# Expert turns of a mixture of experts: seven on 64-row blocks with unsplit weights, third weights unsplit in all, a third set of weight buffers

## The chip, the cores and the metric

The kernel runs on one core of one Trainium2 chip. The metric is the device time of one execution in microseconds (us); the time given for the kernel before is the median of three runs.

## The reference

One inference step through two trunk layers for 512 prompt tokens and 64 sample tokens (8 sequences of 8), 576 tokens of 1,024 features in all. A layer is a mixer (three head groups) with a norm, and then a hierarchical mixture of experts with a second norm. The change touches the experts alone:

```python
def hier_moe(h, l, p):
    ...
    combine = jnp.sum(jax.nn.one_hot(expert_idx, MOE_EXPERTS, dtype=F32) * w_top[..., None], 1)
    hid = jax.nn.silu(jnp.einsum('nd,edf->nef', t, p['moe_w1'][l])) * \
        jnp.einsum('nd,edf->nef', t, p['moe_w3'][l])
    y = jnp.einsum('nef,efd->nd', hid * combine[..., None].astype(hid.dtype), p['moe_w2'][l])
```

There are 16 experts; every token goes to two of them. An expert's weights are w1 and w3 (1,024 x 256 each) and w2 (256 x 1,024), 1 MB apiece in float32. How many tokens an expert gets follows from the inputs, and can be counted by evaluating the reference on them: in layer 0 the experts have 41, 7, 50, 12, 11, 106, 60, 143, 99, 48, 186, 103, 75, 25, 64 and 122 tokens, in layer 1 they have 3, 4, 9, 10, 31, 64, 82, 3, 13, 70, 88, 15, 76, 215, 291 and 178.

## The kernel before, in words

**Work.** `experts` (L1660 on) runs the experts of a layer one after the other, in 16 turns b = 0 to 15. Turns 0 and 1 are experts 0 and 1; the others come by rank, in the order of `RANK`, a table that sets light experts between full ones. Turn 2 holds the fullest of the others, turns 5 and 8 the next two. A turn's `Block` takes up to 128 tokens' rows. An expert with more than 128 tokens has a second block `b2` on the same weights, one with more than 256 a third, `b3`; these stand under `tc.If`, and every engine branches round them when they aren't needed. By the counts above, second blocks run in turns 2 and 5 of layer 0 and in turns 2, 5 and 8 of layer 1, and one third block in turn 2 of layer 1: 18 blocks in layer 0 and 20 in layer 1.

**A block's steps.** `gather` (L1301, POOL's queue): an indirect DMA fetches the rows. `turn` (L1313): PE transposes them in eight pieces, ACT (L1316) and DVE (L1317) write them as a pair of float32r tiles, high and low part. `up(0)`, `up(1)` (L1324): the products with w1 and w3; each takes 24 matmuls of 256 columns, since both sides are pairs: high x high, high x low and low x high, over 8 pieces of 128 features. ACT's silu (L1326) closes `up(0)`, a DVE product (L1328) `up(1)`. `hid` (L1334): two transposes, and a pair again (L1336, L1337). `down` (L1348 to L1350): 12 matmuls of 512 columns with w2's pair, then ACT (L1354) and DVE (L1356) write the weighted rows to `ys`. `scatter` (L1360, POOL's queue): an indirect DMA adds the rows to `ybuf` in DRAM. Scatters of one expert may overlap; a scatter waits for that of the expert before, since both may add to the same row.

**Weights.** Each 1 MB piece is loaded by SP (`expert_piece`, L1270) and split into a pair by ACT (L317, high part) and DVE (L318, low part):

```python
split.hi = act.activation(hi[:, :n], raw[:, :n], AF.Copy)
dve.tensor_tensor(lo[:, :n], raw[:, :n], hi[:, :n].bitcast(F32), op=ALU.subtract)
```

There are two sets of three raw buffers, `wraw` and `slots`; turns take them alternately. Four places for pairs (pools `wsp`, `w2p`).

**Order.** The loop `for b in range(NE + 1)` in `experts` is a software pipeline: in turn b it issues `up(0)` of b, the split of w2 of b - 1, the load of w2 of b + 1, the split of w1 of b + 1, the loads of w1 and w3 of b + 2, `up(1)` of b, the conditional blocks, `turn` of b + 1, `gather` of b + 2, the split of w3 of b + 1, `down` and `scatter` of b - 1, and `hid` of b. Buffers are double: rows, `ys` and hidden tiles by b % 2. The last two turns' rows take another way to the next norm. `ahead` loads and splits the first weights of the next layer's projection.

Of the kernel before, what the change touches and what calls it, by code (L numbers as in the profile page):

```python
# [44 lines left out]
# second norm: the tiles to which the last two experts' rows come from the chip, all tiles in order  # L45
# [3 lines left out]
# when the groups of the modulation (layer, group) are worked out: beside SSD, GLA, the output projection of either layer  # L49
# [10 lines left out]
def _tables():  # L60
# [46 lines left out]
    # a token's number - 1023, in two parts  # L107
    put("tok", np.stack([np.tile(p[:, None] - 127, (1, 5)), np.tile(128 * np.arange(5) - 896, (128, 1))], 2))
    put("iota384", np.tile(np.arange(384.0), (128, 1)))
    # rows (table, expert): what tells equal counts apart, the expert's own column, ranks of the columns (table, turn), the expert  # L110
# [5 lines left out]
    put("expert", e[:, None])  # L116
    put("iota256", np.tile(np.arange(256.0), (128, 1)))
# [33 lines left out]
def _body(nc, tc, a, ctx, dbg):  # L151
# [16 lines left out]
    class Views:  # L168
        """a pool's tiles as pieces of one tile."""
# [28 lines left out]
    # the last constants are loaded where they are used  # L198
# [31 lines left out]
    # per-layer modulation held feature-major for the mixer input: [f, k, (shift, 1+scale), 9]  # L230
# [8 lines left out]
    def ada_steps(l, g):  # L239
        """one piece of a group's columns after the other."""  # L240
        # quadrants: group 0 (shift, scale) of the mixer; 1 (shift, gate); 2 (scale, gate), the gate that of the columns before
# [19 lines left out]
        if g == 2:  # L261
            # the norm's gain and bias meet the experts' scale and shift
# [11 lines left out]
            # the prompt's, feature-major  # L274
# [506 lines left out]
    def gla(l, gp, q, k, v, la, lac, gates):  # L781
# [1464 lines left out]
```

## Time and profile before

| | |
|---|---|
| median of three runs | 1490.86 us (1490.02 to 1493.58) |
| span of the profiled execution, first to last instruction | 1487.9 us |
| PE busy | 1235.3 us, 83% |
| DVE busy | 1015.5 us, 68% |
| ACT busy | 606.0 us, 41% |
| POOL busy | 499.1 us, 34% |
| DMA moved | 258.50 MB |

Busy time is summed over stages of different kinds, so its share of the whole span doesn't tell what bounds a stage. The experts are read from stretches of the trace: layer 0's lie between 478 and 711.4 us, layer 1's between 1187 and 1440 us. The start of a turn's silu (L1326 on ACT) follows its `up(0)` and serves as a mark of the turn. A group's row gives what it takes, the idle time of the engine before it and what ended that; a granted clock of 1.0 is 2.4 GHz of TensorE, 0.5 is 1.2 GHz.

### The profile page before, as it was taken

What the parts mean: (1) busy time and instruction counts of PE and PEld (TensorE: products, weight loads), DVE (VectorE), ACT (ScalarE), POOL (GpSimd) and SP (SyncE); (2) the same over time, 40 slices, a digit from 0 to 9 for tenths busy, and PEclk for the clock granted to TensorE, in tenths of its full rate; (3) what the DMA queues carried; (4) which work ended last, traced back from release to release, by engine and by line L of the source; (5) the groups of instructions that cost most, each with busy time, mean ns of one, the idle gap of its engine ahead of it and who ended that gap; (6) DMA issues with size and microseconds to landing.
All of it is one profiled execution on the core that took longest, in us unless ns stands there. A gap on an engine that the chain in (4) does not pass through costs nothing. (4 is left out here: it accounts for less than half of the span.)

```text
span 1487.9 us, 23447 instructions
## 1 busy us (share of the span) xinstructions
PE 1235.3 (83%) x8446; PEld 1028.5 (69%) x8446; DVE 1015.5 (68%) x2035; ACT 606.0 (41%) x978; POOL 499.1 (34%) x354
## 2 busy tenths in 40 slices
PE   4999999988985788898489998989998578688870
PEld 0998777775764677787289887767576466677750
DVE  0576466347889867788877647446788965575887
ACT  0552233331354454666355223333134444364742
POOL 0023122224153555342252312233314363633315
PEclk7899999999976899999799998999997698999995
DMA  9545665754231555998624310017543253685952
GB/s 311 164 149 172 239 237 201 282 203 147 95 127 47 199 208 181 310 320 287 180 82 150 116 58 32 30 45 268 167 175 106 83 216 110 211 268 179 340 155 99
DMA packets 93426, 258.50 MB, mean 174 GB/s; under 512 B 25854, under 2 KB 54432, under 8 KB 74328
## 3 DMA queue, kind: packets, MB, share of 16 engines
q1 hardware_dynamic: 82136, 237.66, 45.5%
q0 software_dynamic: 11136, 18.87, 5.5%
q8 instruction: 86, 1.41, 0.4%
q14 instruction: 68, 0.56, 0.1%
HBM read 236.26 MB, written 34.70 MB: 182 GB/s over the span
## 5 line engine op out<-in xcount | busy, mean ns | idle before, releaser
L318 DVE TENSOR_TENSOR wlo<-wraw,whi 128x2048 fp32r<-128x2048 f32 x72 | 180.3, 2509 | 38.8 <-ACT whi L317 36.1
L390 PE MATMUL ps<-whi,hT 128*128 128x256 f32 (+1 forms) x640 | 186.4, 291 | 0.8 <-DVE yi L706 0.8
L391 PE MATMUL ps<-wlo,hT 128*128 128x256 f32 (+1 forms) x640 | 181.1, 283 | 1.0 <-DVE wlo L318 1.0
L392 PE MATMUL ps<-whi,hT 128*128 128x256 f32 (+1 forms) x640 | 181.1, 283 | 0.1
L317 ACT ACTIVATE whi<-wraw 128x2048 fp32r<-128x2048 f32 x72 | 137.8, 1914 | 42.2 <-PEq L1894 9.8
L1360 POOL DMA_INDIRECT ybuf<-ys,srci x34 | 88.2, 2595 | 175.4 <-DVE hidl L1337 35.4
L318 DVE TENSOR_TENSOR wlo<-slots,whi 128x2048 fp32r<-128x2048 f32 x48 | 119.2, 2491 | 16.0 <-ACT whi L317 11.8
L390 PEld LDWEIGHTS ps<-whi,hT 128*128 128x128 f32 (+1 forms) x640 | 115.8, 181 | 13.2 <-issue 10.1
L1324 PE MATMUL ps<-whi,xh 128*128 128x256 f32 x608 | 95.1, 303 | 33.9 <-DVE xl L1317 23.6
L391 PEld LDWEIGHTS ps<-wlo,hT 128*128 128x128 f32 (+1 forms) x640 | 115.6, 181 | 3.6 <-issue 2.1
L392 PEld LDWEIGHTS ps<-whi,hT 128*128 128x128 f32 (+1 forms) x640 | 115.2, 180 | 1.3 <-issue 0.8
L1324 PEld LDWEIGHTS ps<-whi,xh 128*128 128x128 f32 x608 | 83.8, 204 | 38.7 <-DVE xl L1317 25.6
L317 ACT ACTIVATE whi<-slots 128x2048 fp32r<-128x2048 f32 x48 | 92.1, 1918 | 28.5 <-PEq L1883 10.4
L1324 PE MATMUL ps<-whi,xl 128*128 128x256 f32 x608 | 89.9, 292 | 6.2 <-DVE xl L1317 6.1
L1324 PE MATMUL ps<-wlo,xh 128*128 128x256 f32 x608 | 91.8, 297 | 1.1 <-DVE wlo L318 1.1
L380 PE MATMUL ps<-hT,whi 128*128 128x288 f32 x512 | 88.5, 294 | 0.0
L1324 PEld LDWEIGHTS ps<-whi,xl 128*128 128x128 f32 x608 | 82.7, 201 | 7.2 <-DVE xl L1317 7.0
L1324 PEld LDWEIGHTS ps<-wlo,xh 128*128 128x128 f32 x608 | 84.8, 206 | 1.3 <-DVE wlo L318 1.3
L1301 POOL DMA_INDIRECT qk<-hbuf,srci x32 | 48.0, 1499 | 81.9 <-PE ps L1313 55.2
L380 PEld LDWEIGHTS ps<-hT,whi 128*128 128x128 f32 x512 | 74.6, 188 | 0.4 <-ACT zdt L519 0.4
L1482 PE MATMUL ps<-whi,mh 128*128 128x512 f32 (+1 forms) x160 | 71.1, 444 | 3.7 <-ACT mh L1468 3.7
L254 PE MATMUL ada<-wada,scond 128*32 128x512 f32 x384 | 57.2, 670 | 18.3 <-DMA wada<-w_ada 18.3
(526 smaller groups left out, 2942.2 us busy)
## 6 DMA issues: line engine op xcount, KB each, us to landing
wada<-w_ada SPq DMA_DIRECT2D x48, 1024.0 KB
wraw<-moe_w SPq DMA_DIRECT2D x48, 1024.0 KB
slots<-moe_w SPq DMA_DIRECT2D x48, 1024.0 KB
wraw<-w_in SPq DMA_DIRECT2D x24, 1024.0 KB
wraw<-w_out SPq DMA_DIRECT2D x8, 1024.0 KB
ybuf<-bz SPq DMA_DIRECT2D x8, 512.0 KB
slots<-ybuf SPq DMA_DIRECT2D x8, 512.0 KB
slots<-ln SPq DMA_DIRECT2D x6, 512.0 KB
```

Source lines behind the costliest of these rows:

```text
L254: pe.matmul(acc[32 * q:32 * q + 32, :], sc_[:, k, :], w[:, o:o + 512], start=(k == 0), stop=(k == KD - 1))
L317: split.hi = act.activation(hi[:, :n], raw[:, :n], AF.Copy)
L318: dve.tensor_tensor(lo[:, :n], raw[:, :n], hi[:, :n].bitcast(F32), op=ALU.subtract)
L380: pe.matmul(p[:mw, :], lhs[:, k, m0:m0 + mw], rhs[:, k, 288 * h:288 * (h + 1)], start=(k == 0 and lhs is vh and rhs is hT[0]), stop=(k == ...
L390: pe.matmul(p[:n], hT[0][:, k, xs], vh[:, k, :], start=(k == 0), stop=False)
L391: pe.matmul(p[:n], hT[0][:, k, xs], vl[:, k, :], start=False, stop=False)
L392: pe.matmul(p[:n], hT[1][:, k, xs], vh[:, k, :], start=False, stop=(k == KD - 1))
L1301: self.got = pool.indirect_dma_start(out=self.X[r], out_offset=None, in_=hbuf[:, :], in_offset=bass.IndirectOffsetOnAxis(ap=self.tabs[0][r ...
L1324: pe.matmul(p, x[:, k], v[:, k], start=(x is self.xh and v is vh and k == 0), stop=(x is self.xl and k == KD - 1))
L1360: st = pool.indirect_dma_start(out=ybuf[:, :], in_=self.ys[r], in_offset=None, out_offset=bass.IndirectOffsetOnAxis(ap=self.to[r], axis=0) ...
L1482: pe.matmul(p[:n], mh[:, k, :n], vh, start=(k == 0), stop=False)
```

## The change

Turns whose rank is under 2 or over 8, but not the last two, become light: `LIGHT` = turns 0, 1, 3, 4, 6, 7 and 9. The others (2, 5, 8, 10 to 15) stay as they are but for w2.

- A light turn (`class Light`) takes a block of 64 rows. Its weights and rows are plain float32 and not split. `up` has for each of the 8 pieces one matmul with w1, whose result goes to PSUM partitions 0 to 63, and one with w3 into partitions 64 to 127. `down` puts the two halves of the 1,024 output columns side by side in the same way, and one ACT operation over 128 partitions x 512 writes `ys`; the scatter has 128 half rows of 2 KB, by a table of its own (`tabs[3]`, made in `finish` with four small matmuls, one DVE and one ACT operation).
- A light expert with more than 64 tokens has a further 64-row block `bx`, one with more than 128 also the old second and third block, under a `tc.If` in each light turn. By the counts above none of the seven has more than 64 tokens in either layer (turn 9 has exactly 64 in both).
- `down` takes w2 and the hidden rows as plain float32 in every block: 4 matmuls of 512 columns, no split of w2, no L1337.
- A third set of raw buffers, `w3rd`, takes the room of the pair pool `w2p`; turn b takes set b % 3. w1 and w3 of b + 3 are loaded once `up` of a light turn b has read them, those of b + 4 once the heavy turn b + 1 is split, and w2 of b + 2 after `down` of b - 1. Pairs are left with the two places of `wsp`.

```diff
+LIGHT = [b for b in range(NE - 2) if RANK[b] < 2 or RANK[b] > 8]
...
         def up(self, i):
-            vh, vl = [w.rearrange("p (k n) -> p k n", k=KD) for w in self.w[i]]
             p = ps(256, self.pl)
...
-            vh, vl = [w.rearrange("p (f n) -> p f n", f=2) for w in self.w[2]]
+            v = self.w[2].rearrange("p (f n) -> p f n", f=2)
             for h in range(2):
                 c = slice(512 * h, 512 * (h + 1))
                 p = ps(pl=self.pl)
                 for f in range(2):
-                    pe.matmul(p, hh[:, f], vh[:, f, c], start=(f == 0), stop=False)
-                    pe.matmul(p, hh[:, f], vl[:, f, c], start=False, stop=False)
-                    pe.matmul(p, hl[:, f], vh[:, f, c], start=False, stop=(f == 1))
+                    pe.matmul(p, self.hT[:, f], v[:, f, c], start=(f == 0), stop=(f == 1))
...
+    class Light(Block):
...
+        def gather(self, r=None):
+            if not self.part:
+                return super().gather(slice(0, 64))
...
+        def turn(self):
+            p = ps(pl=self.pl)
...
+            for k in range(KD):
+                pe.transpose(p[:, 64 * k:64 * (k + 1)], self.X[0:64, 128 * k:128 * (k + 1)], ident[0:64, 0:64])
+            act.activation(self.xT, p.rearrange("p (k n) -> p k n", k=KD), AF.Copy)
+
+        def up(self):
+            v = [w.rearrange("p (k n) -> p k n", k=KD) for w in self.w[:2]]
+            p = ps(256, self.pl)
+            for k in range(KD):
+                for i in range(2):
+                    pe.matmul(p[64 * i:64 * i + 64], self.xT[:, k], v[i][:, k], start=(k == 0), stop=(k == KD - 1))
+            sl, slp = self.sl[0:64], self.slp[0:64]
+            act.activation(sl, p[0:64], AF.Silu)
+            dve.tensor_tensor(slp.rearrange("p f a -> p a f"), sl.rearrange("p (a f) -> p a f", f=2),
+                              p[64:128].rearrange("p (a f) -> p a f", f=2), op=ALU.mult)
...
+        def down(self):
+            v = self.w[2].rearrange("p (f n) -> p f n", f=2)
+            p = ps(pl=self.pl)
+            for f in range(2):
+                for h in range(2):
+                    pe.matmul(p[64 * h:64 * h + 64], self.hT[:, f, 0:64], v[:, f, 512 * h:512 * (h + 1)], start=(f == 0), stop=(f == 1))
+            act.activation(self.ys[:, 0:512], p, AF.Copy, scale=self.tabs[4][:, self.part, self.col:self.col + 1])
+
+        def scatter(self, r=None):
+            return self.add(ybuf[:, :].rearrange("t (h c) -> (t h) c", h=2), self.ys[:, 0:512],
+                            self.tabs[3][:, self.part, self.col:self.col + 1], 2 * T)
...
+            def room(b):
+                return [wraw.tile([128, 2048], F32, name="wraw", tag="raw") for _ in range(3)] if b % 3 == 0 else (slots[:3], w3rd)[b % 3 - 1][:]
...
             for b in range(NE + 1):
-                if b < NE:
-                    bl[b].up(0)
-                if b > 0:
-                    if b == NE:
-                        bl[b - 1].hi = lambda: pair(w2p)
-                    bl[b - 1].split(2)
-                    if 1 < b + 1 < NE:
-                        load(b + 1, 2)
-                if b + 1 < NE:
+
+                if 0 < b < NE:
+                    if b in LIGHT:
+                        bl[b].up()
+                    else:
+                        bl[b].up(0)
+                if b + 1 < NE and b + 1 not in LIGHT:
+                    raw = bl[b + 1].w
+                    bl[b + 1].w = list(raw)
                     bl[b + 1].split(0)
-                if b + 2 < NE:
-                    bl[b + 2].w = rot()
-                    for i in range(2):
-                        load(b + 2, i)
-                if b < NE:
+                if b < NE and b not in LIGHT:
                     bl[b].up(1)
...
+                if b < NE and b in LIGHT and b + 3 < NE:
+                    for i in range(2):
+                        load(b + 3, i)
                 if b + 1 < NE:
                     bl[b + 1].turn()
                     if b + 2 < NE and b + 2 not in GSPLIT:
                         bl[b + 2].gather()
-                    bl[b + 1].split(1)
+                    if b + 1 not in LIGHT:
+                        bl[b + 1].split(1)
+                        if b + 4 < NE:
+                            for i in range(2):
+                                load(b + 4, i)
...
+                if b == 0:
+                    load(2, 2)
+                elif b + 2 < NE:
+                    load(b + 2, 2)
```

**PE in layer 0, from `hid` of turn 3 to `turn` of block 5, before.** `xh`, `xl` are a block's rows, `whi`, `wlo` a weight's pair, `ps` PSUM, `cst` the identity for a transpose; `qk` holds gathered rows and the product of `up`.

```order
L1334 MATMUL ps<-cst,qk 128x128 x2
L1324 MATMUL ps<-whi,xh_4630 128x256 x8
L1324 MATMUL ps<-wlo,xh_4630 128x256 x8
L1324 MATMUL ps<-whi,xl_4631 128x256 x8
L1324 MATMUL ps<-whi,xh_4630 128x256 x7
L1837 UNCONDITIONAL_BRANCH
L1324 MATMUL ps<-whi,xh_4630 128x256
L1324 MATMUL ps<-wlo,xh_4630 128x256 x8
L1324 MATMUL ps<-whi,xl_4631 128x256 x8
L1313 MATMUL ps<-cst,qk 128x128 x8
```

The 48 matmuls are both `up` products of turn 4.

**The same engine after the change, from `up` of turn 3 to `up` of turn 4.** `xf` are a light block's rows, `wraw`, `slots` and `w3rd` raw weights, `hid` the hidden rows.

```order
L1421 MATMUL ps<-wraw,xf_4637 64x256 x16
L1413 MATMUL ps<-cst,qk 128x64 x8
L1366 MATMUL ps<-w3rd,hid_4638 128x512 x4
L1430 MATMUL ps<-cst,qk 128x64 x2
L1421 MATMUL ps<-slots,xf_4636 64x256 x15
```

Sixteen matmuls on 64 partitions stand in the place of 48, four for the `down` of the heavy turn 2 in the place of twelve. Between `up` of turn 3 and its `hid` stand the transposes of block 4 and the `down` of block 2.

**SP's queue in layer 0, the loads of one turn, before:**

```order
L1270 DMA wraw_5475<-moe_w1 128x2048
L1270 ISA
L1270 DMA wraw_5476<-moe_w3 128x2048
L1837 UNCONDITIONAL_BRANCH
L1270 ISA
L1270 DMA wraw_5477<-moe_w2 128x2048
```

These are the weights of turn 4, w1 and w3 issued in turn 2 and w2 in turn 3. **After the change, those that stand in turn 4:**

```order
L1278 DMA slots_3266<-moe_w1 128x2048
L1278 ISA
L1278 DMA slots_3266<-moe_w3 128x2048
L1903 TENSOR_LOAD ebi_3262
L1903 ISA x2
L1278 ISA
L1278 DMA w3rd_4645<-moe_w1 128x2048
L1278 ISA
L1278 DMA w3rd_4645<-moe_w3 128x2048
L1278 ISA
L1278 DMA wraw_5690<-moe_w2 128x2048
```

Five pieces stand together, for turns 7 (`slots`), 8 (`w3rd`) and 6 (`wraw`), so loads are issued two to four turns ahead of their use; before, it was one to two.

## Rows read from the trace of the kernel before

**Rows 1.** The page's head and part 1: span, busy time and share.
```profile
span 1487.9 us, 23447 instructions
PE 1235.3 (83%) x8446; PEld 1028.5 (69%) x8446; DVE 1015.5 (68%) x2035; ACT 606.0 (41%) x978; POOL 499.1 (34%) x354
```

**Rows 2.** Busy time by stretch: engines' us (instructions), granted clock, DMA share, GB/s.
```profile
478.00:711.40 233.40, 196.45 (x1268) 177.75 (x1266) 178.80 (x148) 129.94 (x139) 100.06 (x44) 0.92 0.72 244
1187.00:1440.00 253.00, 210.00 (x1376) 186.47 (x1375) 172.07 (x152) 128.28 (x144) 105.30 (x45) 0.95 0.65 222
609.80:620.70 10.90, 9.86 (x72) 9.03 (x71) 7.97 (x7) 7.72 (x8) 3.76 (x2) 1.00 1.02 325
640.60:655.10 14.50, 12.20 (x78) 11.20 (x77) 11.24 (x9) 9.61 (x9) 5.79 (x2) 0.88 1.00 354
674.30:691.10 16.80, 12.64 (x72) 11.16 (x72) 12.25 (x12) 9.75 (x9) 1.58 (x1) 0.80 1.01 339
1404.70:1418.70 14.00, 11.07 (x81) 10.07 (x80) 12.20 (x12) 9.63 (x9) 3.38 (x1) 1.00 0.97 341
609.30:702.90 93.60, 85.36 (x582) 77.93 (x581) 77.36 (x67) 63.92 (x66) 31.11 (x15) 0.95 0.92 316
```

**Rows 3.** PE's timeline, one turn of layer 0: start, us, instructions in order.
```profile
609.59 1.11 PE L1324 MATMUL ps<-whi,xh 128*128 128x256 f32 x8
610.54 1.12 PE L1324 MATMUL ps<-wlo,xh 128*128 128x256 f32 x8
611.50 1.12 PE L1324 MATMUL ps<-whi,xl 128*128 128x256 f32 x8
612.46 1.04 PE L1313 MATMUL ps<-cst,qk 128*128 128x128 f32 x8
613.25 0.48 PE L1348 MATMUL ps<-whi,hidh 128*128 128x512 f32 x1
...
616.14 0.38 PE L1334 MATMUL ps<-cst,qk 128*128 128x128 f32 x2
```

**Rows 4.** PE's timeline: plain float32 products in other stages, and their neighbours.
```profile
135.23 1.92 PE L254 MATMUL ada<-wada,scond 128*32 128x512 f32 x16
137.08 1.08 PE L669 MATMUL ps<-cst,ll 64*64 64x64 f32 x15
712.11 5.42 PE L2000 MATMUL ps<-qk,v 128*128 128x512 f32 x12 [0.75 <-DVE qk L1352]
```

**Rows 5.** Groups of layer 0's experts: busy us, mean ns, idle before and releasers.
```profile
L318 DVE TENSOR_TENSOR wlo<-wraw,whi 128x2048 fp32r<-128x2048 f32 x25 | 67.5, 2705 | 5.9 <-ACT whi L317 5.1 <-ACTq L1883 0.9
L318 DVE TENSOR_TENSOR wlo<-slots,whi 128x2048 fp32r<-128x2048 f32 x24 | 58.4, 2445 | 8.7 <-ACT whi L317 7.0 <-ACTq L1883 1.4 <-DVEq L1883 0.2
L317 ACT ACTIVATE whi<-wraw 128x2048 fp32r<-128x2048 f32 x25 | 47.9, 1917 | 15.1 <-PEq L1883 5.1 <-PEq L1894 4.3 <-DMA wraw<-moe_w 4.3
L1317 DVE TENSOR_TENSOR xl<-ps,xh 128x512 fp32r<-128x512 f32 x36 | 23.2, 681 | 5.8 <-ACT xh L1316 5.5 <-DVEq L1883 0.2
```

**Rows 6.** Who PE and ACT waited for, layer 0, then layer 1: us, times, longest.
```profile
PE ps L1324 <- DVE xl L1317: 18.7, 8, 4.7
PE ps L1324 <- DVE xl L1317: 11.0, 10, 2.9
ACT whi L317 <- DMA slots<-moe_w: 7.0, 4, 2.4
```

**Rows 7.** DMA of layer 0's experts, from 478 to 711.4 us.
```profile
DMA packets 13728, 56.90 MB, mean 244 GB/s; under 512 B 3415, under 2 KB 5591, under 8 KB 8317
```

**Rows 8.** POOL's timeline, scatters of layer 0; last, all scatters' time to landing.
```profile
621.90 2.92 POOL L1360 DMA_INDIRECT ybuf<-ys,srci  x1 [7.06 <-DVE hidl L1337]
...
667.40 2.72 POOL L1360 DMA_INDIRECT ybuf<-ys,srci  x1 [6.54 <-DMA ybuf<-ys,srci]
...
702.86 2.79 POOL L1360 DMA_INDIRECT ybuf<-ys,srci  x1 [7.66 <-DMA wraw<-w_in]
DMA to landing us min/median/max: 2.7/8.5/13.3
```

More of the change, by code (lines that the diff above doesn't have):

```diff
@@ L116, in _tables @@
     put("expert", e[:, None])
+    put("beyond", np.tile(np.array([64.0 if b in LIGHT else 128.0 for b in range(NE)]), (128, 1)))
     put("iota256", np.tile(np.arange(256.0), (128, 1)))
@@ L1305, in split @@
         def split(self, i):
[L1306 removed]
+            self.w[i] = split(self.w[i])
         def turn(self):
@@ L1652, in finish @@
             act.activation(wslot, pv[:, :, 1], AF.Copy)
+            p = ps(256)
+            for e in range(2):
+                for h in range(2):
+                    pe.matmul(p[64 * h:64 * h + 64, 32 * e:32 * e + 32], tq[:, 64 * e:64 * e + 64], perm, start=True, stop=True)
+            pv = p[:, 0:64].rearrange("p (j a e) -> p j a e", j=2, a=2)
+            dve.tensor_scalar(tabs[3], pv[:, :, 0], 2.0, C("off"), op0=ALU.mult, op1=ALU.add)
+            act.activation(tabs[4], pv[:, :, 1], AF.Copy)
             held.clear()
@@ L1770, in aside @@
                     for i in range(2):
-                        ahead.load(i)
+                        ahead.load(i, w3rd[i])
                 if b == NE - 2:
@@ L1835, in parts @@
                 h, r = HALF[b], ROWS[b]
-                if h < r and both:
+                if b not in LIGHT and h < r and both:
                     with tc.If((half & (1 << b)) > 0) as big:
@@ L1842, in parts, with whole @@
                 return [f(slice(0, r))]
+            def whole(q, w):
+                q.w = w
+                q.gather()
+                q.turn()
+                for i in range(2):
+                    q.up(i)
+                q.hid()
+                q.down()
+                q.scatter()
             steps = finish(Xs[3])
@@ L1847, in experts @@
             pool.memset(Xs[3], 0.0)
-            with two(0):
-                b2[0].gather()
-                if 0 in SOON:
-                    three(0, b3[0].gather)
             with tc.issue_after(last[0].ins), tc.issue_after(last[1].ins):
-                bl[0].split(0)
-                bl[0].split(1)
+                bl[0].up()
+            for i in range(2):
+                load(2, i)
             for i in range(2):
@@ L1892, in experts @@
                             three(b - 1, more)
-                    if b in at_hand:
+                    if b in at_hand and b in LIGHT:
+                        with two(b):
+                            q = bx[b]
+                            q.w = bl[b].w
+                            q.gather()
+                            q.turn()
+                            q.up()
+                            q.hid()
+                            q.down()
+                            q.scatter()
+                            if b in SECOND:
+                                with tc.If((second & (1 << b)) > 0):
+                                    whole(b2[b], bl[b].w)
+                                    three(b, lambda: whole(b3[b], bl[b].w))
+                    elif b in at_hand:
                         with two(b):
@@ L1939, in experts @@
             wr = slots[1]
-            his = [pair(w2p) for _ in range(2)]
             with tc.If(nx > 0), ExitStack() as sI:
```

137 lines of the change are left out of this document (85 added, 52 removed).

## The prediction

> **What bounds the kernel now.** The page's head [rows 1] says PE 83% busy over the span, but the change touches the two expert stages alone, so I went to busy time by stretch [rows 2]. Layer 0's experts take 233.4 us, layer 1's 253.0 us, a third of the span together. In both PE is the busiest engine (196.45 and 210.00 us), DVE second (178.80 and 172.07 us), and DMA stands at 0.72 and 0.65. The timeline of one turn [rows 3] gives PE's work for a block at full clock: 24 products of a piece start at 609.59 and the transposes follow at 612.46, so 2.87 us a piece and 5.74 us for two; transposes 0.8 us; twelve products of `down` from 613.25 to 616.14, 2.9 us; two transposes of `hid`, 0.25 us. That is 9.7 us. 18 blocks make 175 us in layer 0, 20 make 194 us in layer 1. Some 59 us of either stage are therefore not PE work at full speed, but waits and stretches at half clock.
>
> The plain turn 609.8 to 620.7 [rows 2] shows why a turn isn't shorter: PE 9.86 of 10.90 us, and DMA at a share of 1.02 with 325 GB/s. DVE has three splits of about 2.5 us [rows 5] and some 3 us more in a turn. So PE, DVE and DMA all need about 10 us per turn. Where a turn is longer, it is the weights that are late: 640.6 to 655.1 and 674.3 to 691.1 [rows 2] have DMA at 1.00 and 1.01 with 354 and 339 GB/s, and the granted clock falls to 0.88 and 0.80 (partly at 1.2 GHz) while PE has gaps. Layer 1 has the like at 1404.7 [rows 2]; ACT's splits there waited up to 2.4 us a time for a load [rows 6]. Other gaps of PE are the DVE's: the rows' low part stands behind splits in its queue, 18.7 us in layer 0 and 11.0 us in layer 1 [rows 6]. Last, POOL: a scatter waits for the landing of the one before. The eight from 621.90 to 702.86 [rows 8] stand 11.6 us apart (81 us over seven steps), of which landing takes 8.5 us in the median and up to 13.3.
>
> **What the change takes and adds.**
>
> *PE, light turn.* Plain float32 products cost more than float32r. The 12 matmuls that begin at 712.11 [rows 4] take 5.42 us, 0.44 us apart, and each is one of the two passes that a product of 512 columns takes: 0.87 us a product, and half of that, 0.43 us, for 256 columns. But four 32-column products on parts of the array run side by side: 16 matmuls of 512 columns in 1.92 us at 135.23 [rows 4], where one after the other they would take 7. So I take a pair of 64 columns as one: eight pairs of `up` at 0.43 us are 3.45 us, two pairs of `down` at 0.87 us are 1.73 us, transposes and `hid` 1.0 us; 6.2 us against 9.7, that is 3.5 us less in each of 7 turns, 24.5 us per layer.
> *PE, heavy block.* `down` becomes four products at 0.87 us, 3.5 us against 2.9: 0.6 us more in 11 blocks of layer 0 (nine turns, two second blocks) and 13 of layer 1, 6.6 and 7.8 us. PE's sum: 18 us less in layer 0, 17 in layer 1, 35 together.
> *Mode of the array.* A light turn goes between parts and the whole array about five times, 70 times in all. After the parts' products the next matmul starts at 137.08 [rows 4], 0.09 us after the last pass would have made room (the fourth of four steps of 0.43 us ends at 136.99). I take 0.09 us, 6 us in all; bounds 0 and 0.2 us (the 0.19 us by which the last of the 16 outlasts its step: 1.92 less four steps), so 0 to 14 us. The Trainium skill's page on TensorEngine Tiling (Array Packing), under Key Properties, says that a change of tiling mode drains the engine; this speaks against the change. [...]
> *DVE and ACT.* Of the splits [rows 5], 21 of a layer go with the light turns and 9 with the heavy ones' w2: 30 of 48, at 2.5 us on DVE 75 us and at 1.92 us on ACT 58 us; the light rows' low parts (2 x 0.68 us a block) are 9.5 us more. DVE falls from 179 to about 95 us and ACT from 130 to about 70, both well under PE. A light turn keeps one silu, one product, three copies. What DVE's queue made PE wait can mostly go; I take two thirds of 18.7 and 11.0 us [rows 6], 12 and 7 us, bounds none and all.
> *Loads.* SP's queue has the same 48 pieces, but two to four turns ahead of their use. The late turns named above exceed 9.7 us by 4.8, 7.1 and 4.3 us, and layer 0's start runs at low DMA shares while turns wait. I take 12 us in layer 0 and 10 in layer 1, bounds 0 and 25 each. The cap is DMA itself: 56.9 MB in layer 0 [rows 7] at the 316 GB/s that 93.6 us sustained [rows 2] is 180 us; with some 10 us for the last block behind its weights, layer 0 can't fall under 190 us, 43 us less than now, or at 354 GB/s 171 us, 62 less.
> *POOL.* A light turn's gather has 64 rows; its scatter 128 half rows with the same bytes. Its price isn't in the trace. From below it is 0, since the bytes are the same and no gain follows; from above, 4.8 us more (the 13.3 us of the longest landing [rows 8] against the median's 8.5) for each of 14 light scatters, 67 us, if that chain ended the stage. I take 0, the nearer end, since the chain starts earlier: its first link stands behind turn 0, which no longer waits for splits.
> *No cost.* Six instructions of `finish` for `tabs[3]` and `tabs[4]` are first read by the first scatter, behind a whole turn; if they weren't covered, 1.5 us a layer. The test in each light turn stands where a test of second blocks stood. Second blocks keep their own waits (gather, `ys`, scatters).
>
> Sum: layer 0, 18 + 12 + 12 = 42 us, just under its cap; layer 1, 17 + 7 + 10 = 34 us; 76 us less 6 for the modes is 70. I take off 4 more for the turns in which PE, DMA and the scatter chain now all come out near 640 to 660 us and can't all be met at once: 66 us. The profiled execution spans 1487.9 us, 3 us under the median of 1490.86, which I keep as the offset: **1425 us**. 0.3%, about what a measurement of this kernel can tell from no change, is 4.5 us.
>
> **The rivals.**
> - *The gains lie behind the scatters and the loads.* PE gets its 35 us, but turns now pile against a chain of scatters whose links are 11.6 us [rows 8] and lengthen with more loads in flight. For it: in the second half of layer 0 the links already are as long as a turn, and 667.40 names the landing as what ended POOL's wait. Against it: 16 scatters at 11.6 us, from an earlier start, end no later than PE does. It leaves 20 to 35 us, 1456 to 1471 us; chance 0.14.
> - *The pairs don't run side by side.* The two passes of a float32 product are one instruction's, and the second product of a pair could wait for both. `up` would then take 6.9 and `down` 3.5 us, 11.4 us a light turn, 1.7 more than now; 24 us over 14 turns, and 14 for the heavy `down`: PE gains 38 us of work. With the 6 us for modes, and half of DVE's and the loads' 41 us back, it ends at 1514 us, slower. It decides, with those 20 us, at a light `up` of 5.8 us (and a `down` of half of it). Against it stand the 16 matmuls in 1.92 us [rows 4]. Chance 0.07.
> - *More of the idle time goes than I count.* Of the 59 us in each layer two thirds go, up to the caps: 95 us, 1396 us; chance 0.17.
> - *Light blocks overflow.* A 65th row for turn 9 adds a whole block, some 12 us a layer with its latencies; the counts say 64, which leaves no slack but needs none. Chance 0.02, still faster.
>
> **How the numbers follow.** The forecast has 0.60 and its own range is 1408 to 1450: unknowns of 14 us for modes, 13 for DVE, 25 for loads, not all on one side. For 8 in 10 I reach to 1394, the case of more idle time, and to 1468, inside the scatter case. Faster by over 0.3%: 0.60 + 0.17 + 0.02 and most of the scatter case, 0.91; slower 0.06, nearly all from the pairs; same 0.03.
>
> **What would show it.** The first and the second matmul of each pair starting within 0.02 us of each other, and a light `up` of about 3.5 us; DVE's busy time in layer 0's experts near 95 us; PE's near 180 and still first; hardly a wait of PE for L1317's successor; the stage of layer 0 near 192 us and of layer 1 near 220 us, with DMA's share near 0.9 in layer 0. The prediction is wrong if light turns are over 9 us apart with PE idle (then POOL's waits or loads tell which), if pairs start 0.2 us apart, or if other stages change by more than 5 us.

## The result, and the profile after

The change takes 1446.66 us (median of four runs, 1444.60 to 1451.68) beside 1492.22 us of the kernel before on the same chip: a ratio of 0.9703, 95% interval 0.9677 to 0.9728, some 44 to 46 us faster. The forecast was 1425, its range 1394 to 1468. The sign held and the time lies in the range; the size is two thirds of what was forecast, and a third of it did not come from where the sum put it.

The page's head of the change; [rows 1] are the lines of before:

```profile
span 1449.9 us, 22505 instructions
PE 1206.7 (83%) x8086; PEld 922.8 (64%) x8086; DVE 830.8 (57%) x1903; ACT 490.3 (34%) x906; POOL 444.5 (31%) x354
```

To see where the time went I cut both traces at the same marks: the start of the first and of the last turn's silu in each layer. That leaves out each layer's start and last `down`, so the stretches are shorter than those of [rows 2]. Busy time by stretch; first layer 0's turns, then what lies between the last turn of layer 0 and the first of layer 1, then layer 1's turns (length, then PE, PEld, DVE, ACT and POOL busy, granted clock, DMA share, GB/s). Before:

```profile
486.70:701.10 214.40, 178.72 (x1181) 162.33 (x1180) 162.96 (x134) 119.43 (x129) 94.94 (x40) 0.93 0.74 255
701.10:1187.20 486.10, 414.17 (x2844) 344.17 (x2843) 342.23 (x872) 179.65 (x354) 155.26 (x134) 0.89 0.34 112
1187.20:1429.00 241.80, 199.27 (x1324) 178.31 (x1324) 164.12 (x144) 124.70 (x138) 103.54 (x44) 0.94 0.66 227
```

The change:

```profile
486.90:692.10 205.20, 166.43 (x996) 115.57 (x997) 80.83 (x68) 69.45 (x96) 74.13 (x41) 0.91 0.77 261
692.10:1162.10 470.00, 407.81 (x2852) 336.84 (x2852) 327.63 (x871) 172.25 (x349) 149.29 (x133) 0.91 0.36 118
1162.10:1392.00 229.90, 188.23 (x1128) 131.47 (x1129) 85.53 (x76) 74.58 (x107) 76.27 (x45) 0.92 0.68 233
```

The two spans differ by 38.0 us: 9.2 in layer 0's turns, 16.1 between the layers, 11.9 in layer 1's turns, 1 behind them. (The profiled run of the change was its longest of four, so the spans show some 6 to 8 us less than the medians.) Two readings follow. First, PE's busy time fell by 12.3 and 11.0 us, where the sum had 15 and 14 (18 and 17, less 3 a layer for the modes), and DVE's halved, from 163 to 81 us; but PE's idle time, length less busy, went from 35.7 to 38.8 us in layer 0 and from 42.5 to 41.7 in layer 1, where 24 and 17 us were to go. Second, the largest piece lies where the change touches no line.

PE's timeline of the change shows the new parts as they run (start, us, instructions in order):

```profile
555.31 3.67 PE L1421 MATMUL ps<-wraw,xf 128*64 128x256 f32 x32
558.91 0.71 PE L1413 MATMUL ps<-cst,qk 64*128 64x64 f32 x8
...
615.10 2.56 PE L1345 MATMUL ps<-whi,xh 128*128 128x256 f32 x8 [2.93 <-ACT xh L1332]
617.45 1.91 PE L1345 MATMUL ps<-wlo,xh 128*128 128x256 f32 x8
619.16 1.91 PE L1345 MATMUL ps<-whi,xl 128*128 128x256 f32 x8
...
623.10 1.11 PE L1345 MATMUL ps<-whi,xl 128*128 128x256 f32 x8
635.12 1.97 PE L1326 MATMUL ps<-cst,qk 128*128 128x128 f32 x8 [10.90 <-ACT ys L1370]
...
685.07 1.88 PE L1366 MATMUL ps<-slots,hid 128*128 128x512 f32 x4
687.10 1.95 PE L1366 MATMUL ps<-slots,hid 128*128 128x512 f32 x4 [0.15 <-PEq L1974]
```

A light `up` (32 passes) takes 3.60 us from its first row to the transposes behind it; eight pairs at 0.43 were put at 3.45. A heavy `down` takes two halves of 1.9 us. At 635.12 stands the largest gap of layer 0. Behind the gap of 2.93 us that ends at 615.10 eight products take 2.56 and then 1.91 us (granted clock 0.50 from 615.1 to 620.8), where they take 1.11 at full clock (1.00 at 623): PE came out of that idle stretch at the half clock, so the gap cost more than its own length.

What PE waited for in layer 0's turns, then the first row of layer 1's, and last two rows of layer 1's turns before the change (us in total, times, longest):

```profile
PE ps L1326 <- ACT ys L1370: 10.9, 1, 10.9
PE ps L1326 <- PEq L1985: 5.9, 1, 5.9
PE ps L1366 <- ACT hid L1356: 5.1, 1, 5.1
PE ps L1345 <- ACT xh L1332: 2.9, 1, 2.9
PE ps L1345 <- ACT whi L322: 2.8, 1, 2.8
PE ps L1345 <- DVE xl L1333: 2.6, 3, 1.3
...
PE ps L1438 <- ACT ys L1370: 10.8, 1, 10.8
...
PE ps L1324 <- ACT ys L1354: 8.1, 3, 6.8
PE ps L1348 <- ACT ys L1354: 4.6, 1, 4.6
```

The wait for the rows' low part, 18.7 us in [rows 6], is down to 2.6 (L1333). Three waits have POOL behind them: in layer 0 the gap of 10.9 us and the 5.1 us, both new, and 10.8 us in layer 1, where PE waited 12.7 us (8.1 and 4.6) for ACT's copies into `ys` before the change too. The 5.9 us stand near layer 0's start (at 499.5 us) and were not followed up. For the gap at 624 us, POOL's and ACT's timelines (the latter two rows are ACT's), and then what POOL's queue did at the line of the test, L1974 (shortest, median and longest ns; first and last start):

```profile
618.36 3.68 POOL L1379 DMA_INDIRECT ybuf<-ys,route  x1 [9.55 <-ACTq L1974]
622.34 1.07 POOL L1314 DMA_INDIRECT qk<-hbuf,srci  x1 [0.30 <-issue]
635.93 1.58 POOL L1379 DMA_INDIRECT ybuf<-ys,srci  x1 [12.52 <-ACT qk L1347]
...
615.42 1.91 ACT L322 ACTIVATE whi<-slots 128x2048 fp32r<-128x2048 f32 x1
634.38 0.69 ACT L1370 ACTIVATE ys<-ps,wslot 128x512 f32<-128x512 f32 x1 [17.05 <-DMA qk<-hbuf,srci]
```

```profile
L1974 POOLq EVENT_SEMAPHORE  x3: 43/43/43, 629.7 to 633.5; - x3
L1974 POOLq ALU_OP  x2: 32/32/32, 618.8 to 619.7; - x2
L1974 POOLq INC_SWDGE_SEM  x2: 645/654/664, 619.0 to 633.6; - x2
```

The second test, for turn 9, is reached by POOL at 619.7 and isn't taken. POOL does not go on at once: its waits on the queues' semaphores stand at 629.7 to 633.5, 11 us behind the scatter of 618.36 and the gather of 622.34 that it had just issued, and only then does it count up the semaphore for the transfers that the skipped body would have made (633.6). ACT's copy into `ys`, whose row names the gather's landing and which comes right behind that count, starts at 634.38, and PE's next transposes at 635.12. So this skipped body with transfers in it stopped POOL's queue until what it had just issued had landed. It is the only such stop in the turns of either layer: at every other untaken test in the turns POOL goes on within 2 us, and before the change at all of them.

The gap of 10.8 us in layer 1 looks alike and is something else. ACT's row ahead of it, and what POOL's queue did at L1974 in layer 1's turns:

```profile
1236.59 0.69 ACT L1370 ACTIVATE ys<-ps,wslot 128x512 f32<-128x512 f32 x1 [13.18 <-DMA ybuf<-ys,srci]
...
L1974 POOLq INC_SWDGE_SEM  x5: 1505/1587/1610, 1346.0 to 1383.4; - x5
```

The first untaken test at this line in these turns is counted at 1346.0, more than 100 us later. The copy is that of turn 2's third block. It waits 13.18 us for the landing of a scatter (POOL's at 1225.96), since the turn's three blocks share two `ys` buffers.

### The profile page after: what moved, and what is told of

The parts are those of the page before. It is cut to its first block, busy times and chain, and to the rows that moved or that the text cites. A ratio compares the mean times of both kernels' runs of the same rounds, so it can differ in the third digit from the quotient of the medians.

```text
span 1449.9 us, 22505 instructions
## 1 busy us (share of the span) xinstructions
PE 1206.7 (83%) x8086; PEld 922.8 (64%) x8086; DVE 830.8 (57%) x1903; ACT 490.3 (34%) x906; POOL 444.5 (31%) x354
## 5 line engine op out<-in xcount | busy, mean ns | idle before, releaser
L323 DVE TENSOR_TENSOR wlo<-wraw,whi 128x2048 fp32r<-128x2048 f32 x30 | 68.6, 2287 | 31.8 <-ACT whi L322 31.4
L323 DVE TENSOR_TENSOR wlo<-w3rd,whi 128x2048 fp32r<-128x2048 f32 x22 | 67.4, 3092 | 27.8 <-ACT whi L322 27.8
L1345 PE MATMUL ps<-whi,xh 128*128 128x256 f32 x384 | 62.1, 308 | 22.7 <-ACT whi L322 7.7
L1379 POOL DMA_INDIRECT ybuf<-ys,srci x20 | 32.6, 1632 | 141.0 <-DVEq L1985 36.8
L1560 PE MATMUL ps<-whi,ml 128*128 128x512 f32 (+1 forms) x160 | 66.5, 420 | 3.2 <-DVE ml L1545 3.2
L1366 PE MATMUL ps<-w3rd,hid 128*128 128x512 f32 x128 | 62.8, 635 | 5.5 <-ACT hid L1356 5.1
L1559 PE MATMUL ps<-wlo,mh 128*128 128x512 f32 (+1 forms) x160 | 67.3, 421 | 0.0
L322 ACT ACTIVATE whi<-wraw 128x2048 fp32r<-128x2048 f32 x30 | 57.3, 1910 | 15.7 <-PE ps L386 7.6
L1345 PE MATMUL ps<-wlo,xh 128*128 128x256 f32 x384 | 57.0, 294 | 0.2 <-DVE wlo L323 0.2
L834 POOL TENSOR_TENSOR qh<-qx,ex 128x256 f32<-128x256 f32 x32 | 29.6, 953 | 89.4 <-issue 73.5
```

The costliest lines, as they stand in the source:

```text
L1345: pe.matmul(p, x[:, k], v[:, k], start=(x is self.xh and v is vh and k == 0), stop=(x is self.xl and k == KD - 1))
L1366: pe.matmul(p, self.hT[:, f], v[:, f, c], start=(f == 0), stop=(f == 1))
L1559: pe.matmul(p[:n], mh[:, k, :n], vl, start=False, stop=False)
L1560: o = pe.matmul(p[:n], ml[:, k, :n], vh, start=False, stop=(k == 3))
```

## The theories and the experiments

My theory when I planned the runs (B): the tests in the light turns hold the stages; I then took the gap in layer 1 for a test as well. Beside it stood A, the chain of scatters, which holds ACT's copies through the two `ys` buffers (the 5.1 us), and C, the weights' loads. The table has each run's median, its ratio to the kernel before on the same chip, and, from its one profiled execution, the four lengths in us cut as above. The profiled execution can lie 6 to 7 us off the median (e9's is its slowest, 1480.2; e12's its fastest, 1435.6), so small differences of length prove nothing alone.

| run | median us | ratio, 95% interval | layer 0's turns | between | layer 1's turns | behind |
|---|---|---|---|---|---|---|
| before | 1491 to 1496 by chip | 1 | 214.4 | 486.1 | 241.8 | 58.9 |
| the change | 1446.7 | 0.970 (0.968 to 0.973) | 205.2 | 470.0 | 229.9 | 57.9 |
| e1 third ys | 1446.4 | 0.969 (0.965 to 0.973) | 199.9 | 468.3 | 228.8 | 57.9 |
| e2 no tests | 1463.1 | 0.982 (0.978 to 0.985) | 188.6 | 483.6 | 228.0 | 72.4 |
| e3 both | 1461.1 | 0.979 (0.976 to 0.982) | 186.8 | 482.1 | 229.1 | 73.8 |
| e4 one by one | 1468.5 | 0.985 (0.982 to 0.988) | 205.9 | 472.8 | 236.1 | 57.9 |
| e5 one test | 1455.6 | 0.976 (0.973 to 0.979) | 188.8 | 480.1 | 229.3 | 69.1 |
| e6 late head | 1448.1 | 0.971 (0.968 to 0.973) | 202.8 | 469.8 | 228.9 | 57.9 |
| e7 two sets | 1440.5 | 0.966 (0.963 to 0.969) | 193.3 | 468.1 | 230.4 | 58.1 |
| e8 all heavy | 1487.9 | 0.998 (0.995 to 1.000) | 212.0 | 473.8 | 248.4 | 58.0 |
| e9 spare tile (on before) | 1474.5 | 0.984 (0.980 to 0.988) | 214.3 | 471.9 | 245.5 | 59.9 |
| e10 third plain (on before) | 1463.5 | 0.977 (0.972 to 0.982) | 197.4 | 489.8 | 227.2 | 64.4 |
| e11 two sets, third ys | 1446.4 | 0.967 (0.963 to 0.970) | 195.9 | 468.8 | 234.1 | 58.0 |
| e12 e9 and e10 (on before) | 1442.4 | 0.966 (0.963 to 0.969) | 196.6 | 471.5 | 223.1 | 58.0 |

**e1, a third `ys`.**

```diff
-yss = [ep.tile([128, D], F32, name=f"ys{i}") for i in range(2)]
+yss = [ep.tile([128, (D, D, 512)[i]], F32, name=f"ys{i}") for i in range(3)]
+yb = [2 - b % 3 if b < 10 else 1 - b % 2 for b in range(NE)]
```

> One staging buffer more: ys becomes three (the third of 512 columns, for light turns), so that the copies of a turn into ys wait for the scatter of three turns ago, not two. Nothing else is changed. Theory A (the scatters' chain reaches PE through ys: ACT's copy into ys waits for a scatter two turns back, and the next turn's copies stand behind it in ACT's queue): the 5.1 us gap of PE in layer 0 at 559.6 goes and ACT's waits of ys copies on DMA (some 39 us in layer 0's stage) fall by half or more; 8 to 20 us faster than the change. Theory B (POOL's drain at a test that isn't taken): the two gaps of PE of 10.9 us (layer 0 at 624, layer 1 at 1226) stay, within 4 us of the change. Rival C (the weights' loads set the pace): within 3 us of the change, the same idle time under other names.

Measured: the median did not move (1446.4). In the trace the 5.1 us gap is gone, and ACT's light copies no longer wait for scatters (16.0 us in the change), while the gap at the test stands, 10.75 us long. Layer 0 is 5.3 us shorter. So A is true of that one gap, and taking it away shows in no median. The third buffer serves light turns alone: the wait of turn 2's third block in layer 1 stands in e1 too (10.5 us), so the run doesn't test the chain there.

**e2, no tests in the light turns.**

```diff
-at_hand = [e for e in (b - 1, b, b + 1) if e in SECOND and e not in LIGHT or e == b and b in LIGHT]
+at_hand = [e for e in (b - 1, b, b + 1) if e in SECOND and e not in LIGHT]
...
+with tc.If((beyond & sum(1 << e for e in LIGHT)) > 0):
+    for b in LIGHT:
+        with two(b):
```

> The tests for rows beyond 64 are taken out of the seven light turns and put, with the work they guard, behind the last turn (one outer test, weights loaded again if it is ever taken). Theory B (a test whose body holds gathers and scatters makes POOL wait, when it isn't taken, until the earlier transfers of the queues in that body have landed; everything behind waits): both gaps of PE of 10.9 us go, no wait of POOL over 4 us is left at such a test inside the light turns; 18 to 30 us faster than the change. Theory A (ys and the chain): within 5 us of the change. Rival C (loads): within 3 us of the change, since the weights are as late as before.

Its stretches, the fourth behind layer 1's last turn:

```profile
488.70:677.30 188.60, 162.47 (x997) 115.83 (x997) 79.63 (x68) 69.80 (x97) 73.15 (x40) 0.93 0.83 285
677.30:1160.90 483.60, 410.75 (x2853) 337.51 (x2853) 327.18 (x871) 172.37 (x350) 151.55 (x135) 0.90 0.35 116
1160.90:1388.90 228.00, 189.33 (x1128) 134.99 (x1128) 81.09 (x76) 74.91 (x106) 73.23 (x43) 0.91 0.67 232
1388.90:1461.30 72.40, 20.82 (x58) 9.69 (x56) 43.25 (x85) 14.70 (x20) 25.29 (x10) 0.66 0.23 73
```

Layer 0's turns lose 16.6 us, and PE's idle time there goes from 38.8 to 26.1: B holds in layer 0. In layer 1, where no test had stopped POOL, only 1.9 us go; the gap of 10.84 at 1226 us is down to 3.3, in the order that this program happens to have, and others came (7.5 us at 1297). And the same test behind the last turn costs 14.5 us at the end and about as much at layer 0's, so the whole is 16 us slower than the change. My total was wrong: I had not priced the place the test was moved to.

**e3, both.** The edits of e1 and e2 together.

> e1 and e2 together: three ys buffers and no tests in the light turns. If A and B are both right and separate, the gains add: 28 to 45 us faster than the change, PE's idle time in layer 0's stage from 39 us to 15 or less. If the chain of scatters itself is what is left, the stage of layer 0 stays above 18 links of 10.5 us, 190 us, and the gain is smaller than the sum. If C holds, within 5 us of the change.

186.8 us in layer 0, PE idle for 26.3: hardly more than e2 alone. The gains do not add: in e2 ACT's light copies still wait 18.3 us for scatters, but none of PE's waits in layer 0 is longer than 3.3 us, so a third buffer has little to give back there.

**e4, the products of a pair one by one.**

```diff
-for k in range(KD):
-    for i in range(2):
+for i in range(2):
+    for k in range(KD):
         pe.matmul(p[64 * i:64 * i + 64], self.xT[:, k], v[i][:, k], start=(k == 0), stop=(k == KD - 1))
```

(and `down` likewise)

> The two products of a pair are no longer issued in turn: first all eight steps of one, then all eight of the other, in up and in down, so that two that follow one another write the same half. The light turn's up should take 6.9 us instead of 3.45 and down 3.5 instead of 1.7, 5.2 us more per light turn, 73 us over 14 turns if all of it stood on the path. If light turns are held by scatters and tests (A, B), about 25 to 45 us of it shows in the total; if PE bounds the light turns, 60 to 75; if loads hold them (C), under 20.

PE's timeline, a light `up` and the row behind it:

```profile
563.48 6.32 PE L1421 MATMUL ps<-wraw,xf 128*64 128x256 f32 x32
569.73 0.71 PE L1413 MATMUL ps<-cst,qk 64*128 64x64 f32 x8
```

6.25 us instead of 3.60, where I had expected 6.9: the pairs do run side by side. The time rises by 22 us, between C's case (under 20) and that of A and B (25 to 45), so the size decides nothing between them. Layer 0's turns hardly grow (205.9 against 205.2): PE's 12.7 us more of work went into idle time (38.8 to 26.8), so PE did not hold the light turns there.

**e5, one test behind the last turn.** The edit against e2:

```diff
-with tc.If((beyond & sum(1 << e for e in LIGHT)) > 0):
+with tc.If(nx + (beyond & sum(1 << e for e in LIGHT)) > 0):
     for b in LIGHT:
...
-with tc.If(nx > 0), ExitStack() as sI:
+    with tc.If(nx > 0), ExitStack() as sI:
```

> e2 again, but its outer test behind the last turn and the test for blocks beyond an expert's third, which stood there before, are one: one test, with both bodies under it. e2 took 16.6 us off layer 0's stage and 2 off layer 1's, and lost some 14 us at each layer's end, where the change has one test and e2 two. Theory B (each untaken test with transfers in its body is a stop, wherever it stands): the 14 us at each end go, the stages keep e2's gain, about 1428 us (1422 to 1436). If the 14 us come from the larger body or from loads that are issued behind it rather than from the second test, the end stays long and the time is 1440 to 1463.

1455.6: the ends stay long (69.1 against 57.9). So it is not the second test. In the change PE's first products of the combination, and DVE's sum of them at 1406 us, come before POOL's last scatter is issued; in e5 that sum stands at 1409, behind the test and the loads issued after it, with a gap of 9 us ahead; PE's first product there waits 10.7 us, for a scatter's landing by its row. POOL's own stop at the end's test is no longer than the change's (4.7 us in both). So what stands behind the test in the order seems to cost the time, not the stop itself; no run parts this from the larger body.

**e6, the head of layer 1's projection late again.**

```diff
-ahead.load(i, w3rd[i])
+ahead.load(i)
```

> One part of the change undone: the first two weight pieces of layer 1's input projection are loaded into the ring of weight buffers again, as before, and not into the third set. The change gained some 16 us between layer 0's last turn and layer 1's first, where no line was changed. Theory D (these pieces come earlier, and the order of layer 1's mixers follows): 10 to 18 us slower than the change, all of it between the stages. Rival (the order there and the clock granted differ for another reason): within 4 us of the change.

No difference: theory D falls, the 16 us between the layers are not these loads.

**e7, two sets of weights.** (`[wraw...]` stands for three tiles of `wraw`.)

```diff
-return [wraw...] if b % 3 == 0 else (slots[:3], w3rd)[b % 3 - 1][:]
+return [wraw...] if b % 2 == 0 else slots[:3]
...
-load(b + 3, i)
+load(b + 2, i)
```

> One part of the change undone: two sets of weight buffers, each piece loaded into the set of two turns before; light blocks and unsplit third weights stay. The prediction priced the loads that come earlier at 12 and 10 us. If that holds: 15 to 30 us slower than the change, with ACT's and PE's waits for weights back. If the turns are held by tests and scatters, and the weights were in time anyway: under 8 us slower.

```profile
486.50:679.80 193.30, 160.48 (x996) 111.88 (x996) 75.38 (x68) 70.22 (x97) 71.16 (x42) 0.94 0.82 285
...
1147.90:1378.30 230.40, 186.51 (x1128) 130.95 (x1128) 78.50 (x76) 74.84 (x106) 75.41 (x44) 0.91 0.68 236
```

The prediction's term does not show: without the third set the kernel is by the medians 6 us faster (the intervals overlap), layer 0's turns 11.9 us. PE waits 6.0 us for w2 there and 2.3 us in layer 1, half and a quarter of the 12 and 10 us. POOL stops at turn 9's test here as well (9.9 us from 611.8), but PE stood waiting for a w2 in that time (5.7 us) and the gap of 10.9 us doesn't come. So the shorter layer 0 is in part the order's doing; in this kernel the third set is worth nothing that can be measured.

**e8, all turns heavy**, with unsplit third weights and the third set. Turn 0's start is rewritten for a heavy block (not shown).

```diff
-LIGHT = [b for b in range(NE - 2) if RANK[b] < 2 or RANK[b] > 8]
+LIGHT = []
```

> No turn is light: all 16 turns are on 128 rows with split first and second weights; unsplit third weights and the third set of buffers stay, and there are no tests in light turns. PE has 4.1 us more in each of 14 turns than in the change (9.7 + 0.6 against 6.2), 57 us. If PE bounded the light turns, 1495 to 1505 us, slower than before. If light turns are held by tests (some 17 us in layer 0) and by scatters (B, A), the light blocks are worth much less than 57 us: 1465 to 1485 us.

```profile
494.20:706.20 212.00, 187.06 (x1116) 145.76 (x1115) 115.31 (x99) 95.37 (x114) 75.88 (x41) 0.94 0.75 252
...
1180.00:1428.40 248.40, 205.93 (x1249) 160.82 (x1248) 125.70 (x107) 100.14 (x124) 80.24 (x44) 0.96 0.65 214
```

1487.9, above what B and A allowed (1465 to 1485): given the third set, the light blocks are worth 41 us. But the gain between the layers is there without them as well (473.8). All eight variants so far have it: from PE's first product with `las` in the mixers (at 839.0 us before) to layer 1's first silu they take 332 to 338 us, the change 332, before 348. (In e2, e3 and e5 the test at layer 0's end hides it in the table.) In the change and all eight PE's rows of layer 1's mixers stand in one order, which differs from before in 17 places of 620 rows. What all share is the PSUM tile that `finish` now takes for `tabs[3]` and `tabs[4]`, one more in the ring that the mixers use. Theory E is that this tile alone turns the order:

**e9, a spare PSUM tile in the kernel before.**

```diff
+            if l == 0:
+                p = ps(256)
+                pe.matmul(p[:, 0:32], tq[:, 0:128], perm, start=True, stop=True)
+                dve.tensor_copy(tq[:, 0:32], p[0:80, 0:32])
             held.clear()
```

> The kernel before, and in layer 0 one product of 32 columns into one PSUM tile more, copied out to a place that is cleared right after (the change's finish has such a tile more). It is of no use but shifts the ring of PSUM tiles by one, and with that PE's rows of layer 1's mixers stand word for word as in the change and its variants, not as before (17 places in 620 rows differ). Theory E (the order of layer 1's mixers, not the experts, gave the 16 us there): 12 to 18 us faster than before, all of it between layer 0's last turn and layer 1's first; both expert stages within 4 us of before. Rival F (those mixers gain because the experts ahead of them are other ones: the clock granted, the loads): within 4 us of before.

```profile
486.90:701.20 214.30, 180.29 (x1182) 163.20 (x1181) 162.96 (x134) 119.68 (x129) 91.72 (x40) 0.92 0.75 256
701.20:1173.10 471.90, 405.97 (x2845) 339.38 (x2844) 336.17 (x872) 179.66 (x355) 151.79 (x134) 0.91 0.35 115
1173.10:1418.60 245.50, 203.52 (x1326) 182.63 (x1325) 163.72 (x144) 124.62 (x139) 101.99 (x44) 0.92 0.65 223
```

A useless product makes the kernel before 1.6% faster. Between the layers 14.2 us go, layer 0's turns stay (214.3), layer 1's are 3.7 us longer. Theory E holds: PE's rows of the mixers now stand in the change's order, that order gave those 14 to 16 us, and the experts have no part in it. That it is the tile, and not the product and the copy that go with it, is argued: all three came together. Which of the moved rows saves the time stays open.

**e10, unsplit third weights alone, in the kernel before.** Two sets, four places for pairs, no light turns. The load of w2 moves behind `down` of the turn before, as its split is gone.

```diff
-pe.matmul(p, hh[:, f], vh[:, f, c], start=(f == 0), stop=False)
-pe.matmul(p, hh[:, f], vl[:, f, c], start=False, stop=False)
-pe.matmul(p, hl[:, f], vh[:, f, c], start=False, stop=(f == 1))
+pe.matmul(p, hh[:, f], v[:, f, c], start=(f == 0), stop=(f == 1))
...
-bl[b - 1].split(2)
```

> The kernel before with unsplit third weights alone: down in plain float32, no splits of w2, hid copied once; two sets, no light turns, and the mixers' rows as before. By the prediction's terms PE gets 0.6 us more a block, 11 us in layer 0 and 12 in layer 1, and the queues of DVE and ACT lose 16 splits a layer, of whose waits two thirds were to go, 12 and 7 us: 1490 to 1500 us. If DVE's waits were never behind the w2 splits, or return under another name: 1505 to 1520. If the splits held more than PE's rows showed: under 1485.

Its stretches, and what is left of PE's wait in layer 0:

```profile
487.00:684.40 197.40, 181.31 (x1117) 142.36 (x1117) 125.53 (x102) 92.95 (x114) 91.22 (x40) 0.97 0.78 271
684.40:1174.20 489.80, 417.40 (x2838) 346.51 (x2837) 338.84 (x870) 177.94 (x353) 156.07 (x134) 0.89 0.35 113
1174.20:1401.40 227.20, 202.64 (x1248) 158.69 (x1248) 127.05 (x110) 96.05 (x123) 95.23 (x44) 0.98 0.69 237
```

```profile
PE ps L1324 <- DVE xl L1317: 4.0, 3, 2.0
```

1463.5, in the lowest of my cases (under 1485) and far under the 1490 to 1500 that the prediction's terms gave. PE is busy 2.6 and 3.4 us longer, yet the turns are 17.0 and 14.6 us shorter, more than the whole change gains there (9.2 and 11.9). (The kernel's end is 5.5 us longer here; e12 has not got that.) PE's idle time falls from 35.7 to 16.1 us and from 42.5 to 24.6, and the granted clock stands at 0.97 and 0.98, where the change has 0.91 and 0.92.

**e11, e7 and e1 together.** The edits of both.

> e7 and e1 together, the version that should beat both kernels: light blocks, two sets of weights, three ys buffers. e7 alone gave 1440.5 us, e1 alone did not differ from the change. If ys holds PE back only where the third set has brought loads forward: 1437 to 1442 us. If third buffer and sets are separate: 1430 to 1437. If the order that the planner finds for light tests decides (e7's layer 0 has no stop of 10.9 us, the change's and e1's have one), the stop may come back and the time is 1443 to 1450.

1446.4, 0.967: no better than e7, within its interval. The third `ys` for light turns is no gain in any mix.

**e12, e9 and e10 together.**

> e10 and e9 together: the kernel before with unsplit third weights and the spare PSUM tile in layer 0, so that layer 1's mixers stand in the change's order; no light turns, two sets of weights. If the two are separate, e10's stages (197 and 227 us) stay and the 14 us between them come on top: by spans 1466 less 14, 1448 to 1453 us in the run's time, by the ratios 0.977 times 0.984, some 1435 to 1440. Either way it is at or under the whole change (1446.7), and light blocks and third buffers have then brought nothing together. If it comes out over 1456, unsplit thirds and the order share a gain, and the light blocks hold the rest.

```profile
484.60:681.20 196.60, 180.25 (x1116) 141.46 (x1116) 125.04 (x102) 92.95 (x114) 89.73 (x40) 0.98 0.80 272
681.20:1152.70 471.50, 408.43 (x2837) 340.69 (x2836) 334.52 (x870) 177.97 (x353) 152.00 (x134) 0.91 0.36 118
1152.70:1375.80 223.10, 199.37 (x1248) 156.51 (x1247) 126.02 (x110) 96.00 (x123) 97.04 (x44) 0.99 0.70 242
```

1442.4, a ratio of 0.966: as fast as the whole change, by the medians 4 us faster, with no light block and no third set. The two parts are separate and add, within the intervals (0.977 times 0.984 is 0.961). With e7 (1440.5) it is the best version found; the intervals of the two and of the change overlap at their edges, so the order among them is not settled, while all three are well below before.

## Why the prediction was right, and where its sum was not

*PE, light turn and heavy block:* right in kind, a fifth too large. The pairs run side by side (e4), `up` takes 3.60 us at full clock, but PE's busy time fell by 12.3 and 11.0 us, not 15 and 14: over layer 0's stage (478 to 703 us) the seven `up` average 4.0 us and the seven `down` 2.7 (28.1 and 19.2 us in all) against 3.45 and 1.73, since some run at the half clock. *Mode of the array:* the transposes behind a light `up` start 0.15 us after its eight pairs of 0.43 us would end (3.45 us behind 555.31, next row 558.91); 0.09 was taken, 0.2 the bound. The Trainium skill's page TensorEngine Tiling (Array Packing), under Key Properties, says that a change of tiling mode drains the engine; whatever drain there is costs no more than that here.

*DVE and ACT:* mis-sized, and the largest error on the good side. The forecast let two thirds of the rows' low part wait go, 12 and 7 us, with "none and all" (18.7) as bounds. That wait did go, and more: with the w2 splits alone gone, e10 shows 19.6 and 17.9 us less idle time, though PE's work is heavier; 14.7 and 4.8 of it stand under the name of the rows' low part. What the sum missed is that PE's granted clock rose as its gaps went: 0.93 became 0.97 and 0.94 became 0.98.

*Loads:* wrong. 12 and 10 us were taken for weights that come two to four turns ahead. e7 takes that away and is no slower. The late turns of [rows 2], with DMA at a share of 1.0, had little to gain by asking earlier, and to make room for the third set the pairs were cut to two places, which the sum did not price. e8 and e12 both have 16 heavy turns, unsplit third weights and the new order; e8 has the third set and two places for pairs, e12 two sets and four places, and they are 45 us apart (10 of it ahead of the first silu, which comes at 494.2 in e8 and at 484.6 in e12). How much of this is the set, the places or turn 0's start was not tried alone and stays open.

*POOL, 0:* right for the light turns' chain (e1), wrong for what stands in POOL's queue. The chain does hold turn 2's three blocks in layer 1, by 10.8 us, as it did before (12.7). *No cost*, "the test in each light turn stands where a test of second blocks stood": this step failed in layer 0. The tests' bodies hold gathers and scatters, and the skipped body of turn 9 stops POOL for 14 us until what it had issued has landed. That stop stands in the change, e1, e4 and e6 (13.6 to 14.5 us) and, shorter, in e7 and e11 (9.8 to 9.9); without the tests layer 0 is 16.6 us shorter (e2).

*Other stages:* the prediction said that it would be wrong if they moved by more than 5 us. They moved by 16. The six instructions of `finish` were named and priced at nothing, as work that is covered; they were covered (the first silu of layer 0 comes at 486.9 us, before at 486.7), but with their PSUM tile the order of layer 1's mixers turned (e9).

So of the 66 us forecast, the turns gave 21 by the profiles, and 16 came from the order, which no term of the sum foresaw: that the time lies well inside the range is in part luck. Without the order it would be near 1463 us. That is the case of the rival "the gains lie behind the scatters and the loads" (1456 to 1471), though in layer 0 by another cause than it named, a test. Against e8 the light blocks took 20.6 and 17.7 us off PE's busy time, where that run's expectation has 29 a layer (4.1 us in each of seven turns), and other costs took most of it back: the stop at turn 9's test, and what came with the third set and the lost places for pairs, which no run parts. e12, without light blocks, is as fast.

## What to carry to other kernels

Price a part by its own experiment before adding the next: here the smallest part (no split of w2) was worth more in the turns than all of them together. For every test that is added, look at the transfers in its body and at what the queue issued just ahead of it: at one of them POOL stood 14 us, until a scatter and a gather had landed, at the others in the turns not over 2 us. A gap that looks the same can have another cause, as in layer 1, so read the waits at each. And where a planner orders the program, compare its order also in the stages that no edit touches, since a few instructions more in one stage can turn it in the next.

## What the runs showed of the hardware

A split on DVE beside POOL's products of `x` (L1846, L1847) takes twice as long. POOL's rows of the change, and DVE's row of the same time, two splits:

```profile
489.10 2.38 POOL L1846 TENSOR_TENSOR x<-x,slots 128x1024 f32<-128x1024 f32 x1
491.55 4.28 POOL L1847 TENSOR_TENSOR x<-x,slots 128x1024 f32<-128x1024 f32 x1
...
489.15 8.83 DVE L323 TENSOR_TENSOR wlo<-w3rd,whi 128x2048 fp32r<-128x2048 f32 x2 [1.17 <-ACT whi L322]
```

8.83 us for two, where the splits of `wraw` and `slots` take 2.29 us each in the same stage. POOL's own second product takes 4.28 instead of 2.38: by these times the two engines take turns, each held for the other's whole instruction. The Trainium skill says in SBUF — State Buffer, under "Who interferes with whom", that a DVE instruction with two inputs in SBUF contends with a GpSimd instruction that reads SBUF, and that contention for the shared ports is an exclusive lock. The trace agrees. It is not new in the change: before, eight splits that ran beside such products in layer 0 took 3.1 to 4.9 us, which is why the mean split of [rows 5] lies at 2.45 and 2.7 us.

The granted clock was the other surprise: 0.91 in the change's layer 0 and 0.98 in that of e12, which has more PE work and fewer gaps. A cheaper block that leaves PE waiting was paid for in products behind it at 1.2 GHz, as at 615.10.
